# A two-layer hybrid decoder trunk on one core: the last weight sum of the seven-product jobs is made on VectorE instead of by accumulating transfers

## The chip, the cores and the metric

The kernel runs on one core of one Trainium2 chip. The metric is the device time of one execution in microseconds; lower is better. Three runs of the kernel before took 1253.19, 1253.20 and 1253.69 us, the median is 1253.2 us. A separate execution was taken with the hardware profiler.

## The reference

Two layers over a sequence of 256 tokens of width 1024, all in 32-bit floats. A layer normalizes h, makes one wide projection, runs retention (four heads) and a state-space scan (four groups) on its parts, projects both back, merges them by sigmoid gates, projects again and adds to h; a SwiGLU feed-forward of width 2816 follows. Cut to the products that matter here:

```python
u = h @ w_in                          # q, k, v, g_ret, z, xbc, dt, gate_ret, gate_ssd
yr = silu(g_ret) * norm(retention(rotary(q), rotary(k), v));  o_ret = yr @ ret_out
ys = norm((ssd_scan(...) + d_skip * xs) * silu(z)) * ssd_norm_w;  o_ssd = ys @ ssd_out
h = h + (sigmoid(gate_ret) * o_ret + sigmoid(gate_ssd) * o_ssd) @ w_o
gate, up = split(rmsnorm(h) @ w_gate_up)
h = h + (silu(gate) * up) @ w_down
```

## The kernel before, in words

**Weights in two parts.** Every large product is made in a 32-bit format of reduced precision, so each operand is split into a high part and a remainder, and three matmuls stand for one (`mm3`, lines 543 to 545). A weight piece is 128 rows by 1024 columns of numbers (512 KB). It is brought by a transfer from SyncE's queue (line 488) into one of four `raw` buffers, ScalarE copies it to `wh` (line 506), VectorE makes `wl = raw - wh` (line 527), and TensorE uses both. Seven pairs of `wh` and `wl` exist, so the splits run at most seven pieces ahead of TensorE. A piece of a plain job feeds 12 matmuls, a piece of a seven-product job 6.

**Seven products.** Some jobs compute a product of two matrices, cut into 2 x 2 blocks, by seven block products in place of eight. Besides the blocks 11, 22 and 21 of the weights they need four sums: t1 and t2 (made one after the other in the buffer of block 11), t3 (in the buffer of block 12) and t4, which adds block 21 to what t2 left. Each block is two pieces, so each sum is made twice in a job. The order of the products is 11, t1, t2, 22, t3, 21, t4, with the pieces of the job's other products (`"*"`) between them. Which sums are made by an accumulating transfer is said by `added`: for a name in it, `plus` calls `add` (line 416), in which GpSimd issues a transfer that reads block 21 again from memory and adds it to the buffer; for a name not in it VectorE adds the piece that is already on the chip (`tt`, line 230), and the piece's own buffer is freed only after that sum.

**The jobs.** Each layer has six such jobs: one for the state-space gate (`gs`, t3 added by transfer), the retention's out projection (`ret`, buffers called `dec`), the state space's (`ssd`), two gate-and-up jobs of the feed-forward and the down projection (buffers called `raws`, blocks 12 in `cc`). Around them stand plain jobs (`z`: 512 columns of the gate of the state space) and jobs in which the weight is the stationary operand (`fm`, lines 988 to 991).

**What sets the order.** The kernel plans itself while it is built: `Flow` runs all streams through a timetable with a cost for each operation, and the instructions are written to each engine in the order that this gives. A line that changes a stream can therefore move instructions of every engine. On the chip each engine works through its own list, and semaphores hold it until operands are there.

Of the kernel before, what the change touches and what calls it, by code (L numbers as in the profile page):

```python
# [192 lines left out]
def trunk_kernel(  # L193
# [58 lines left out]
    def pooled(pool_, shape, dt, tag, bufs):  # L252
        sem = Sem(bufs)
        return sem, lambda name=tag: pool_.tile(list(shape), dt, tag=tag, name=name, bufs=bufs)
# [5 lines left out]
    ccS, new_cc = pooled(tp, (P, D), F32, "cc", 2)  # L260
# [33 lines left out]
    AMID = ("*", "*", "*", "*", "11", "*", "t1", "*", "t2", "22", "*", "t3", "*", "21", "*", "t4")  # L294
# [4 lines left out]
    RMID = ('*', '*', '*', '*', '*', '*', '11', '*', 't1', 't2', '22', 't3', '21', 't4')  # L299
    RET_FIRST, RET_APART, RET_PR = (decS, new_dec), (), 0.0  # L300
# [5 lines left out]
    def group(*adds):  # L306

        of = len(jobs)
        got_turns, got_specs, stars = [], [], []
        for add in adds:  # L310
            t, f, at = add(of)
            if stars:

                t, f = ([(stars[i] if i < len(stars) else 1.0 + i, v) for i, (_, v) in enumerate(e)] for e in (t, f))
            stars = stars or at
            got_turns += t
            got_specs += f
        for into, got in ((turns, got_turns), (specs, got_specs)):
            for _, v in sorted(got, key=lambda e: e[0]):
                if into is turns and turns:  # L320
                    v.before = turns[-1]
                into.append(v)

    def plain(*runs):

        def add(of):
            got_turns, got_specs, n = [], [], sum(len(srcs) for srcs, _ in runs)
            for srcs, apart in runs:
                evs = []
                for i, (src, k, m) in enumerate(srcs):  # L330
                    ev, turn, at = Event(), Turn(), (len(got_turns) + 0.5) / n
                    evs.append(ev)
                    got_turns.append((at, turn))
                    slot = (bigS["D"], new_raw_big) if of == 0 and i < 4 else (rawS, new_raw)
                    got_specs.append((at, (src, k, m, of, slot,
                                           splitter(turn, k, m, ev, of, src if i in apart else None, slot[0]))))
                jobs.append(evs)
            return got_turns, got_specs, []
        return add
# [19 lines left out]
    def sevens(w1, w2, added=("t3",), order=ALONE, slots=None, first=None):  # L359

        def add(of):
            evs = {q: [Event(), Event()] for q in order if q != "*"}
            turn = {(q, i): Turn() for q in evs for i in range(2)}
            at = {(q, i): (2 * order.index(q) + i + 0.5) / (2 * len(order)) for q, i in turn}
            held = {(q, i): Event() for q in ("11", "12", "22", "21") for i in range(2)}
            part = {q: [w[k + i] for i in range(2)]
                    for q, k, w in (("11", 0, w1), ("12", 0, w2), ("22", 2, w2), ("21", 2, w1))}  # L370
            zS, new_z = slots or (rawS, new_raw)
            got_specs = []
            for q, need, sl in (("11", ("11",), first or (segS, new_raw_seg)), ("12", ("t1", "t3"), (zS, new_z)),
                                ("22", ("t2", "22"), (rawS, new_raw)), ("21", ("21",), (rawS, new_raw))):
                need = [c for c in need if c not in added or c not in ("t1", "t2")]
                for i in range(2):
                    land = holder(held[q, i])
                    if (q, i) == ("11", 1):
                        land = then(land, [wino_sums(i, of, evs, turn, held, part, added, zS, (first or (segS,))[0]) for i in range(2)])
                    got_specs.append((min(at[c, i] for c in need) - (0.01 if q == "12" else 0),  # L380
                                      (part[q][i], 2, 512, of, sl, land)))
            jobs.append(evs)
            return ([(at[c], turn[c]) for c in turn], got_specs,
                    [(i + 0.5) / len(order) for i, q in enumerate(order) if q == "*"])
        return add
# [7 lines left out]
    def holder(ev):  # L393
        def land(raw, landed):
            yield landed
            fl.set(ev, raw)
        return land

    def then(land, gens):
        def run(raw, landed):  # L400
            for g in gens:
                fl.spawn(g)
            yield from land(raw, landed)
        return run
# [56 lines left out]
    def tm_srcs(w, kper=2):  # L461

        n = w.shape[2] // 2
        return [(w[k // 2][:, (k % 2) * n : (k % 2 + kper) * n], kper, n) for k in range(0, 8, kper)]

    def fm_srcs(w):
        return [(w[i], 4, 256) for i in range(2)]

    def gate_up_srcs(l, c):
        return [tm_srcs(w_gate_up[l, b, c]) for b in range(2)]  # L470

    def gf_srcs(l, c):
        return [fm_srcs(w_gf[l, n + b]) for n in gf_at(c) for b in range(2)]

    def out_srcs(w):
        return [(w[k0 : k0 + P, :], 1, D) for k0 in range(0, w.shape[0], P)]
# [580 lines left out]
    def out_wino(op, nk, at, tag, order, post, add, ops):  # L1057
# [74 lines left out]
        for t in range(NT):  # L1132
# [8 lines left out]

    FFN = [[("plain", 0)],
           [("fm", 1)],
           [("seven", (2,), ("t3", "t4"))],
           [("fm", 3)],
           [("seven", (4,), ("t3", "t4"))],
           [("fm", NPAIR)]]
    DIRECT = ()
    DOWN_APART = ()
# [15 lines left out]
    def add_layer_jobs(l):  # L1165
        def srcs_of(kind, *at):
            if kind == "gr":
                return tm_srcs(w_gr[l, at[0]])
            if kind in FM:
                return fm_srcs(w_fm[l, FM[kind] + at[0] + (at[0] + at[1] if len(at) > 1 else 0)])  # L1170
            if kind in ("ret", "ssd", "wo"):
                return out_srcs({"ret": ret_out, "ssd": ssd_out, "wo": w_o}[kind][l])
            return tm_srcs(w_tm[l, TM[kind] + at[0]], kper=1 if l == 0 and (kind, *at) == ("v", 0) else 2)

        def adds_of(kind, *at, order=MIXED):
            if kind == "seven":
                c = TM[at[0]] + at[1]
                return [sevens(w_tm[l, c], w_tm[l, c + 1], added=at[2], order=order, slots=None)]
            return [plain((srcs_of(kind, *at), APARTS.get((kind, *at), ())))]

        for m in MIXERS[l]:
            if m == ("ret",):
                group(sevens(w_rw[l, 0], w_rw[l, 1], added=("t3", "t4"), order=RMID, first=RET_FIRST),
                      plain((out_srcs(ret_out[l])[8:], RET_APART)))
            elif m == ("ssd",):
                group(sevens(w_sw[l, 0], w_sw[l, 1], added=("t3", "t4"), order=SMID, slots=(ccS, new_cc)),
                      plain((out_srcs(ssd_out[l])[8:], ())))
            elif isinstance(m, tuple):
                for add in adds_of(*m, order=ALONE):
                    group(add)  # L1190
            else:
                group(*(chain(*(a for j in stream for a in adds_of(*j))) for stream in m))
        for members in FFN:
            adds = []
            for kind, *at in members:
                if kind == "seven":
                    adds.append(chain(*(sevens(w_gate_up[l, 0, c], w_gate_up[l, 1, c], added=at[1], order=ALONE if len(members) == 1 else ASIDE,
                                               slots=(ccS, new_cc)) for c in at[0])))
                elif kind == "fm":
                    adds.append(plain(*((srcs, APART) for c in at for srcs in gf_srcs(l, c))))  # L1200
                else:
                    adds.append(plain(*((srcs, APART) for c in at for srcs in gate_up_srcs(l, c))))
            group(*adds)
        lone = [s for k, s in enumerate(out_srcs(w_down[l])) if k // 4 not in (DW, DW + 1)]
        group(sevens(w_dw[l, 0], w_dw[l, 1], added=("t3", "t4"), order=AMID, slots=(ccS, new_cc)),
              plain((lone, DOWN_APART)))

    def params(l, done):
# [852 lines left out]
    for l in range(DEPTH):  # L2061
        add_layer_jobs(l)
# [158 lines left out]
```

## Time and profile before

| | |
|---|---|
| median of the runs | 1253.2 us |
| the profiled execution | 1253.21 us |
| its span, first to last instruction | 1251.4 us |
| TensorE busy (matmuls) | 1241.9 us, 99% |
| VectorE busy | 1108.2 us, 89% |
| ScalarE busy | 882.7 us, 71% |
| GpSimd busy | 71.1 us, 6% |
| transfers | 266.27 MB, mean 213 GB/s |
| software queue (GpSimd's transfers) | 27.38 MB, 11.8% of the 16 engines' time |
| granted TensorE clock | 0.999 of 2.4 GHz |

Busy time is the time in which an engine had an instruction in work. TensorE's matmuls are pipelined and their ends are modelled, so its 99% says that it was hardly ever without work, not that each matmul was as short as can be. The chain of waits goes back from the last instruction to whatever released each step. In a timeline row the first number is the start, the second the time until the end of the last of the xN instructions.

### The profile page before, as it was taken

How to read it: one execution, taken by the hardware profiler on the slowest of the kernel's cores; microseconds unless marked ns; L12 is line 12 of the kernel's file. 1: busy time of each engine (PE TensorE's matmuls, PEld its weight loads, DVE VectorE, ACT ScalarE, POOL GpSimd, SP SyncE). 2: the span in 40 equal slices, each digit the busy share in tenths (PEclk: the TensorE clock that was granted, in tenths of full speed). 3: DMA queues.
4: the chain of work that ended last, by engine and by line, in shares of the span. 5: the costliest groups of instructions: out<-in, count | busy, mean ns of one | idle time of the engine just before them, and what ended most of it. 6: DMA issues, size and time to landing. Idle time of an engine off the chain costs nothing.

```text
span 1251.4 us, 17609 instructions
## 1 busy us (share of the span) xinstructions
PE 1241.9 (99%) x6286; PEld 1052.4 (84%) x6286; DVE 1108.2 (89%) x1516; ACT 882.7 (71%) x1305; POOL 71.1 (6%) x92
## 2 busy tenths in 40 slices
PE   9999999999999999999999999999999999999997
PEld 8889888888888888888888898888888888888886
DVE  6998989789999979999788888888899998899995
ACT  6866876977776666776586676878877674776753
POOL 0000000001012001001000000000010110010000
PEclk9999999999999999999999999999999999999999
DMA  8758555456768658877776475555577786688872
GB/s 293 248 146 284 184 180 174 153 194 192 253 238 226 229 178 231 297 212 219 249 257 227 124 256 167 188 172 163 208 186 234 243 234 213 225 209 249 289 204 86
DMA packets 76343, 266.27 MB, mean 213 GB/s; under 512 B 8768, under 2 KB 9024, under 8 KB 76256
## 3 DMA queue, kind: packets, MB, share of 16 engines
q1 hardware_dynamic: 68416, 237.25, 55.7%
q0 software_dynamic: 7552, 27.38, 11.8%
q8 instruction: 49, 0.80, 0.2%
q10 hardware_dynamic: 288, 0.52, 0.1%
q14 instruction: 38, 0.31, 0.1%
HBM read 262.96 MB, written 2.16 MB: 212 GB/s over the span
## 4 chain that ended last, share of the span: by engine, by line
PE 92%; ACT 3%; issue 2%; DMA 1%; DVE 0%; POOL 0%; SPq 0%; POOLq 0%; ACTq 0%
PE acc L543 19%; PE acc L544 19%; PE acc L545 19%; PE acc L988 15%; PE acc L989 9%; PE tr L640 2%; PE yps L1700 2%; PE acc L991 2%; ACT wh L506 1%; ACT seg L1668 1%; PE acc L1422 1%; PE tr L1593 1%; PE ips L1687 1%; DMA raw<-in_w_tm_dram 1%; DMA raw<-in_w_gr_dram 0%
## 5 line engine op out<-in xcount | busy, mean ns | idle before, releaser
L506 ACT ACTIVATE wh<-raw 128x1024 fp32r<-128x1024 f32 (+2 forms) x388 | 397.0, 1035 | 150.6 <-PE acc L545 36.3
L527 DVE TENSOR_TENSOR wl<-raw,wh 128x1024 fp32r<-128x1024 f32 (+2 forms) x388 | 458.9, 1196 | 48.5 <-ACT wh L506 46.6
L988 PE MATMUL acc<-xT,wh 128*128 128x512 f32 x840 | 304.2, 400 | 0.0
L989 PE MATMUL acc<-xT,wl 128*128 128x256 f32 x960 | 251.6, 281 | 0.0
L543 PE MATMUL acc<-wh,xT 128*128 128x512 f32 (+1 forms) x568 | 220.6, 388 | 0.0
L545 PE MATMUL acc<-wh,xT 128*128 128x512 f32 (+1 forms) x568 | 216.1, 380 | 0.0
L544 PE MATMUL acc<-wl,xT 128*128 128x512 f32 (+1 forms) x568 | 216.1, 380 | 0.0
L989 PEld LDWEIGHTS acc<-xT,wl 128*128 128x128 f32 x960 | 181.2, 189 | 10.1
L988 PEld LDWEIGHTS acc<-xT,wh 128*128 128x128 f32 x840 | 158.0, 188 | 32.2
L544 PEld LDWEIGHTS acc<-wl,xT 128*128 128x128 f32 x568 | 106.7, 188 | 20.4 <-issue 1.2
L543 PEld LDWEIGHTS acc<-wh,xT 128*128 128x128 f32 x568 | 106.7, 188 | 19.8 <-issue 1.6
L545 PEld LDWEIGHTS acc<-wh,xT 128*128 128x128 f32 x568 | 106.6, 188 | 19.5
L506 ACT ACTIVATE wh<-raws 128x1024 fp32r<-128x1024 f32 x80 | 83.5, 1056 | 31.7 <-DVE raws L230 12.5
L527 DVE TENSOR_TENSOR wl<-raws,wh 128x1024 fp32r<-128x1024 f32 x80 | 96.4, 1222 | 8.9 <-ACT wh L506 8.7
L543 PE MATMUL acc<-wh,A 128*128 128x512 f32 x224 | 89.8, 401 | 0.2
L545 PE MATMUL acc<-wh,A 128*128 128x512 f32 x224 | 87.4, 390 | 0.0
L544 PE MATMUL acc<-wl,A 128*128 128x512 f32 x224 | 87.3, 390 | 0.0
L233 DVE SCALAR_TENSOR_TENSOR cc<-cc,cv 128x255 f32<-128x255 f32 (+1 forms) x144 | 67.3, 479 | 3.0 <-ACT cc L223 2.1
L543 PE MATMUL acc<-wh,C 128*128 128x512 f32 (+1 forms) x152 | 59.2, 389 | 0.0
L544 PE MATMUL acc<-wl,C 128*128 128x512 f32 (+1 forms) x152 | 58.3, 384 | 0.2 <-DVE wl L527 0.2
L545 PE MATMUL acc<-wh,C 128*128 128x512 f32 (+1 forms) x152 | 58.2, 383 | 0.0
L223 ACT ACT_TABLE_LOAD x41 | 52.6, 1283 | 6.1 <-DVE cc L233 5.4
(197 smaller groups left out, 2006.8 us busy)
## 6 DMA issues: line engine op xcount, KB each, us to landing
raw<-in_w_tm_dram SPq DMA_DIRECT2D x104, 512.0 KB, 4.2
raw<-in_w_fm_dram SPq DMA_DIRECT2D x80, 512.0 KB, 4.3
raw<-in_w_gf_dram SPq DMA_DIRECT2D x40, 512.0 KB, 4.5
raw<-in_w_gate_up_dram SPq DMA_DIRECT2D x32, 512.0 KB, 5.8
raw<-in_w_down_dram SPq DMA_DIRECT2D x28, 512.0 KB, 4.5
raw<-in_w_gr_dram SPq DMA_DIRECT2D x24, 352.0 KB, 3.7
seg<-acs SPq DMA_DIRECT2D x16, 512.0 KB, 4.9
raw<-in_ret_out_dram SPq DMA_DIRECT2D x16, 512.0 KB, 4.3
```

The lines of the kernel that those rows point to most:

```text
L223: return Op("act", cost, lambda: nc.scalar.activation(out=out, in_=in_, func=func, **kw), pr, TABLES.get(func))
L233: return Op("dve", 1.04 * n + 130, lambda: nc.vector.scalar_tensor_tensor(out=out, in0=in0, scalar=scalar, in1=in1, op0=op0, op1=op1), pr)
L506: nc.scalar.activation(out=wh[:, :m], in_=raw[:, :m], func=AF.Copy)
L527: nc.vector.tensor_tensor(out=wl[:, :m], in0=raw[:, :m], in1=wh[:, :m].bitcast(F32), op=ALU.subtract)
L543: nc.tensor.matmul(ps, lhsT=lh, rhs=rh, start=first, stop=False, **kw)
L544: nc.tensor.matmul(ps, lhsT=lh, rhs=rl, start=False, stop=False, **kw)
L545: nc.tensor.matmul(ps, lhsT=ll, rhs=rh, start=False, stop=last, **kw)
L640: nc.tensor.transpose(out=ps[:, j * P : (j + 1) * P], in_=src[:, j * P : (j + 1) * P], identity=ident)
L988: nc.tensor.matmul(a, lhsT=wh[:, k % 4, fsl], rhs=x[:, k % 4, :, :], start=k == 0, stop=False)
L989: nc.tensor.matmul(a[:, :SEQ], lhsT=wl[:, k % 4, fsl], rhs=xh[:, k % 4, :], start=False, stop=False)
L991: nc.tensor.matmul(a, lhsT=wh[:, k % 4, fsl], rhs=x[:, k % 4, :, :], start=False, stop=True)
L1700: nc.tensor.matmul(ps[:, i * HD : (i + 1) * HD], lhsT=sg[:, i, :], rhs=xdt[:, i * HD : (i + 1) * HD], start=True, stop=True)
```

## The change

In four of the six seven-product jobs of a layer t4 leaves the tuple `added`: the two gate-and-up jobs, the retention's out projection and the down projection. The state space's out projection keeps both, and the gate job of the state space had t3 alone already.

```diff
     FFN = [[("plain", 0)],
            [("fm", 1)],
-           [("seven", (2,), ("t3", "t4"))],
+           [("seven", (2,), ("t3",))],
            [("fm", 3)],
-           [("seven", (4,), ("t3", "t4"))],
+           [("seven", (4,), ("t3",))],
            [("fm", NPAIR)]]
...
             if m == ("ret",):
-                group(sevens(w_rw[l, 0], w_rw[l, 1], added=("t3", "t4"), order=RMID, first=RET_FIRST),
+                group(sevens(w_rw[l, 0], w_rw[l, 1], added=("t3",), order=RMID, first=RET_FIRST),
                       plain((out_srcs(ret_out[l])[8:], RET_APART)))
...
-        group(sevens(w_dw[l, 0], w_dw[l, 1], added=("t3", "t4"), order=AMID, slots=(ccS, new_cc)),
+        group(sevens(w_dw[l, 0], w_dw[l, 1], added=("t3",), order=AMID, slots=(ccS, new_cc)),
               plain((lone, DOWN_APART)))
```

The 16 transfers of t4 go from GpSimd's list, and VectorE's has 16 sums more. The planner moves other instructions too; TensorE's work is the same, some of it in another order.

VectorE in the first layer's retention out projection, before (-) and after (+): `dec` are the buffers of blocks 11, `raw` of the others, `seg`, `tail`, `xdt`, `yps` belong to the state-space scan that runs beside it, `O` and `sx` take the results.

```order
 L527 TENSOR_TENSOR wl<-raw,wh 128x1024
+L230 TENSOR_TENSOR dec<-dec,raw 128x1024
 L230 TENSOR_TENSOR tail<-tail,xdt 128x512
 L230 TENSOR_TENSOR O<-sx,D 128x512
...
+L230 TENSOR_TENSOR dec<-dec,raw 128x1024
+L527 TENSOR_TENSOR wl<-raw,wh 128x1024 x2
+L527 TENSOR_TENSOR wl<-dec,wh 128x1024 x2
 L230 TENSOR_TENSOR sx<-acc,sx 128x512
...
-L230 TENSOR_TENSOR seg<-seg,cbm 128x1024
```

The two sums come right after the last piece of t3, ahead of the splits of block 21 and of t4; the seg product moves behind the first four splits of the next job.

TensorE at the transposes of the first z result (`tr`), a job later, before:

```order
1556 L543 MATMUL acc_3474<-wh_3442,xT_342 128x512
1557 L544 MATMUL acc_3474<-wl_3457,xT_342 128x512
1558 L545 MATMUL acc_3474<-wh_3442,xT_342 128x512
1559 L640 MATMUL tr_3540<-cst_78,sil_3450 128x128 x4
1560 L543 MATMUL acc_3482<-wh_3442,xT_342 128x512
```

and after:

```order
1557 L545 MATMUL acc_3457<-wh_3440,xT_342 128x512
1558 L1700 MATMUL yps_3522<-xdt_3438,seg_3147 128x64 x8
1559 L543 MATMUL acc_3462<-wh_3440,xT_342 128x512
1560 L544 MATMUL acc_3462<-wl_3454,xT_342 128x512
1561 L545 MATMUL acc_3462<-wh_3440,xT_342 128x512
1562 L640 MATMUL tr_3542<-cst_78,sil_3447 128x128 x4
```

The scan's products `yps` stood earlier and are now just ahead of the transposes, which come three matmuls later.

VectorE in the first layer's down projection, from the second t2 sum's neighbours on (`raws` of blocks 11, `cc` of blocks 12, `O` is h), before:

```order
727 L527 TENSOR_TENSOR wl_5771<-raw_5575,wh_5752 128x1024
728 L527 TENSOR_TENSOR wl_5782<-raws_5490,wh_5763 128x1024
729 L527 TENSOR_TENSOR wl_5794<-raw_5553,wh_5773 128x1024
730 L527 TENSOR_TENSOR wl_5802<-raw_5686,wh_5786 128x1024
731 L527 TENSOR_TENSOR wl_5816<-cc_5513,wh_5797 128x1024
732 L527 TENSOR_TENSOR wl_5827<-cc_5520,wh_5804 128x1024
```

and after:

```order
732 L527 TENSOR_TENSOR wl_5775<-raw_5581,wh_5765 128x1024
733 L230 TENSOR_TENSOR O_3857<-O_3857,sx_5770 128x512
734 L527 TENSOR_TENSOR wl_5790<-raws_5509,wh_5777 128x1024
735 L527 TENSOR_TENSOR wl_5800<-raw_5563,wh_5788 128x1024
736 L527 TENSOR_TENSOR wl_5810<-raw_5679,wh_5795 128x1024
737 L527 TENSOR_TENSOR wl_5821<-cc_5525,wh_5805 128x1024
738 L527 TENSOR_TENSOR wl_5833<-cc_5532,wh_5814 128x1024
739 L230 TENSOR_TENSOR raws_5501<-raws_5501,raw_5786 128x1024
740 L527 TENSOR_TENSOR wl_5847<-raw_5741,wh_5828 128x1024
741 L527 TENSOR_TENSOR wl_5857<-raw_5786,wh_5835 128x1024
```

The first t4 sum stands behind the splits of t2, 22 and t3; an update of h has moved ahead of the second t2 split.

## Rows read from the trace of the kernel before

**Rows 1.** The page: TensorE's busy time, and the chain that ended last.
```profile
PE 1241.9 (99%) x6286; PEld 1052.4 (84%) x6286; DVE 1108.2 (89%) x1516; ACT 882.7 (71%) x1305; POOL 71.1 (6%) x92
...
PE 92%; ACT 3%; issue 2%; DMA 1%; DVE 0%; POOL 0%; SPq 0%; POOLq 0%; ACTq 0%
```

**Rows 2.** The waits of TensorE: us in total, times, longest us.
```profile
PE idle L2094 <- DVE mhalf L2071: 1.3, 1, 1.3
PE tr L640 <- DVE sil L233: 0.6, 2, 0.3
PE acc L544 <- DVE wl L527: 0.2, 1, 0.2
```

**Rows 3.** Groups by line and shape: busy us, mean ns, idle before.
```profile
L230 DVE TENSOR_TENSOR raws<-raws,raw 128x1024 f32<-128x1024 f32 x28 | 34.2, 1222 | 0.4 <-DMA raw<-in_w_tm_dram 0.4
...
L416 POOL DMA_DIRECT2D raws<-in_w_gate_up_dram x8 | 6.9, 863 | 32.1 <-DVE wl L527 21.3 <-DVE sx L230 10.8
```

**Rows 4.** Issues of transfers: KB each, median us from issue to landing.
```profile
raws<-in_w_gate_up_dram POOLq DMA_DIRECT2D x8, 512.0 KB, 5.5
...
raws<-in_w_dw_dram POOLq DMA_DIRECT2D x4, 512.0 KB, 6.7
```

**Rows 5.** Busy us in stretches: PE, PEld, DVE, ACT, POOL; clock, DMA share, GB/s.
```profile
290.00:366.00 76.00, 76.00 (x371) 63.15 (x370) 74.51 (x93) 55.07 (x79) 6.80 (x10) 1.00 0.72 221
496.00:518.00 22.00, 22.00 (x104) 18.45 (x103) 22.00 (x24) 17.96 (x22) 0.88 (x1) 1.00 0.83 244
...
600.00:620.00 20.00, 20.00 (x90) 16.57 (x89) 15.34 (x15) 12.05 (x13) 0.00 (x0) 1.00 0.78 259
```

**Rows 6.** Timeline of VectorE, retention's out projection and z: start us, us, [idle before].
```profile
315.34 0.69 DVE L230 TENSOR_TENSOR tail<-tail,xdt 128x512 f32<-128x512 f32 x1
316.55 0.69 DVE L230 TENSOR_TENSOR O<-sx,D 128x512 f32<-128x512 f32 x1 [0.52 <-PE acc L544]
...
329.49 0.69 DVE L230 TENSOR_TENSOR O<-acc,D 128x512 f32<-128x512 f32 x1 [0.17 <-PE acc L545]
...
335.05 4.63 DVE L527 TENSOR_TENSOR wl<-raw,wh 128x1024 fp32r<-128x1024 f32 x4
...
348.82 1.42 DVE L233 SCALAR_TENSOR_TENSOR sil<-sil,rz,wb 128x512 f32<-128x512 f32 x2
```

**Rows 7.** Timeline of TensorE where those results are used.
```profile
337.68 0.39 PE L544 MATMUL acc<-wl,xT 128*128 128x512 f32 x1
...
350.85 0.60 PE L640 MATMUL tr<-cst,sil 128*128 128x128 f32 x4
```

**Rows 8.** Block 21 in the retention's job, 309 to 313 us: its transfers.
```profile
L488 SPq DMA_DIRECT2D raw<-in_w_rw_dram x2: 327/328/328, 310.1 to 312.4; - x2
L416 POOL DMA_DIRECT2D dec<-in_w_rw_dram x1: 863/863/863, 311.5 to 311.5; - x1
...
DMA to landing us min/median/max: 4.4/6.8/7.0
```

**Rows 9.** Timeline of VectorE, a gate-and-up job and the down projection.
```profile
497.31 1.23 DVE L527 TENSOR_TENSOR wl<-raw,wh 128x1024 fp32r<-128x1024 f32 x1
...
568.45 1.23 DVE L230 TENSOR_TENSOR raws<-raws,cc 128x1024 f32<-128x1024 f32 x1 [1.93 <-DMA cc<-in_w_dw_dram]
...
590.03 1.23 DVE L527 TENSOR_TENSOR wl<-raws,wh 128x1024 fp32r<-128x1024 f32 x1
...
601.70 2.45 DVE L527 TENSOR_TENSOR wl<-raw,wh 128x1024 fp32r<-128x1024 f32 x2 [1.82 <-ACT wh L506]
```

**Rows 10.** Timeline of TensorE where these splits are used.
```profile
504.14 0.39 PE L544 MATMUL acc<-wl,D 128*128 128x512 f32 x1
...
592.49 0.39 PE L543 MATMUL acc<-wh,D 128*128 128x512 f32 x1
592.72 0.39 PE L544 MATMUL acc<-wl,D 128*128 128x512 f32 x1
```

## The prediction

> **What bounds the kernel now.** Read first the busy shares and the chain of waits on the page, then what TensorE waited for, then VectorE's groups, and last the timelines of the places where the change puts work. The profiled execution took 1253.21 us, its span is 1251.4, so 1.8 us lie around the span; the median of the runs is 1253.2, the same. TensorE is busy for 1241.9 us and the chain that ended last is 92% TensorE, 3% ScalarE and 0% VectorE [rows 1]. TensorE's named waits are three rows, 1.3 + 0.6 + 0.2 = 2.1 us, and the largest is the start [rows 2]. So the kernel is bound by TensorE's own work, which the change leaves alone. There is hardly a wait to win back. Time can be lost where VectorE, already full in stretches (74.51 of 76 us at the retention's out projection, 22.00 of 22 in a gate-and-up job) [rows 5], delivers a split weight later than TensorE asks for it. The question is therefore one of margins: how long before its first use each split weight is ready.
>
> **The change part by part.** Four jobs of each layer are touched: the retention's out projection, the two gate-and-up jobs and the down projection. Each has two t4 sums, so 2 x 4 x 2 = 16.
>
> Removed: 16 accumulating transfers of 512 KB, each issued by GpSimd in 0.86 us [rows 3] and landing 5.5 to 6.7 us after the issue (medians) [rows 4]. That is 8.4 MB of queue traffic and 13.8 us of GpSimd. Neither engine nor queue stands in TensorE's waits [rows 2], so I cost the removal at nothing; at most it can return part of those 2.1 us.
>
> Added: 16 VectorE sums of 1.22 us (the same instruction stands there for t2, `raws<-raws,raw`, mean 1222 ns) [rows 3], 16 x 1.222 = 19.6 us by duration. Back to back one occupies the engine for less: four splits of 1.23 take 4.63 us [rows 6], a pitch of (4.63 - 1.23) / 3 = 1.13. So a job gets 2.27 us of VectorE, all jobs 18.2 us. Its cost on the path is between 0 (all inside the margins) and 18.2 us (none); I take the margins of each place.
>
> Retention's out projection. The thinnest margin is the first weight of the next job: its split is the first of the four that start at 335.05, ready at 336.28, and TensorE takes it at 337.68 [rows 6, 7], a margin of 1.40. In the new order two sums come in ahead of it and one seg product, also of 1024 elements, goes behind it, net one pitch, 1.13 us. Two idle pieces of VectorE in that stretch end on TensorE's results, not on VectorE's own lateness: 0.52 before 316.55 and 0.17 before 329.49 [rows 6]. TensorE's schedule doesn't move, so the sums fill them. Net lateness 1.13 - 0.52 - 0.17 = 0.44, margin left 0.96, cost 0. If nothing filled them the lateness is 1.13, still inside 1.40; if the seg product had stayed in front as well, it is 2.27, and the stall is 0.87.
>
> Then the z jobs. The transposes of the first z result stand on TensorE at 350.85, and the two multiplications that feed them run from 348.82 to 350.24, the first done about 349.5 [rows 6, 7], a margin of about 1.3. Behind the four splits the seg product has been made up for, so VectorE is late by up to 2.27 - 0.69 = 1.58; the new TensorE order puts three more products ahead of these transposes, at 0.23 each (592.49 to 592.72) [rows 10] 0.69 us. Margin left 1.3 + 0.69 - 1.58 = 0.4, cost 0; with all 2.27 late, 0.3 of a stall.
>
> The gate-and-up jobs. After t2's splits the weight of product 22 is ready at 497.31 + 1.23 = 498.54 and used at 504.14 [rows 9, 10]: margin 5.6, and 2.27 goes into it. The t4 piece itself gains, since its sum no longer waits 5.5 us for a landing. Cost 0; the fm job behind it has only two weights to split and lets VectorE catch up.
>
> The down projection. The second t2 split starts at 590.03, is ready at 591.26 and used at 592.72 [rows 9, 10]: margin 1.46, the second thinnest place. The new t4 sums stand behind all t2, 22 and t3 splits, so they don't touch it; only one 512-wide update of h (0.69, as such updates take in the retention's stretch) [rows 6] comes ahead of it, margin left 0.77. Behind it VectorE now idles for 1.82 before 601.70 [rows 9] and for 4.66 of the 20 us from 600 to 620 (15.34 busy) [rows 5], which takes the 2.27. Cost 0.
>
> The sum is 1253.2 + 0 for eight jobs. Two places in each layer are left with under a microsecond by estimates that are good to about as much; I add 0.1 us for each of these four, 0.4 in all: **1253.6 us**.
>
> **One place where a rule is weighed.** The two pieces of w21 in the retention's job were issued at 310.1 and 312.4, with an accumulate between them; one of these three transfers took 4.4 us to land, the others 6.8 and 7.0 [rows 8]. The Trainium skill (DMA: Bandwidth & Descriptors, section SWDGE vs HWDGE vs iDMA) says that software-generated and hardware-generated transfers feed different queues of each DMA engine, which serves them in turn. By that rule the second plain transfer becomes faster without the accumulate beside it, near 4.4 us, and the sum stays as it is; by the row as it stands rival A gains. In numbers from rows: with 4.4 us the second piece is there at 316.8, with 6.8 at 319.2. The first new sum takes the place at 315.34, two updates of 512 follow (0.69 each) [rows 6], and the second sum is reached at 315.34 + 1.13 + 0.69 + 0.69 = 317.85, after the one landing and 1.35 us before the other. I take 4.4, as the accumulate is the only transfer that goes.
>
> **The rivals.**
>
> A, slower: the sum waits at the head of VectorE's queue. VectorE runs its queue in order, and a sum whose second operand has not landed holds every split behind it: the first t1 sum of the down projection had it idle for 1.93 us until a landing [rows 9]. The Trainium skill (TensorE: Matmul & The Clock Gate, section Architectural detail: the array is 16x 32x32) calls VectorE's queue a strict first-in, first-out; that row agrees. Place: the second t4 sum in the retention's job, and VectorE's lateness out of the second gate-and-up job running into the down projection. Price: in the retention 1.13 + 1.35 = 2.48 late (the idle pieces then move along) against 1.40, a stall of 1.08 a layer; in the down projection 2.27 brought along against 0.77, 1.50 a layer. Retention alone: 1253.2 + 2.2 = 1255.4; down projection alone: 1253.2 + 3.0 = 1256.2; both: 1258.4. It decides from a lateness of 1.40 and 0.77 us. For it: the full VectorE and the 6.8 us landing. Against it: the accumulate that shared the queue is gone, and the 1.93 idle ahead of the down projection swallows most of a lateness of 2.27.
>
> B, slightly slower: the splits hold, but VectorE's other results come late through the z jobs (the 0.4 us margin above, and the state-space results whose TensorE work moves by up to 6 us in the new order). Price: 0.3 to 1.2 us a layer, 1253.8 to 1255.6. For it: TensorE's row for tr already waits on VectorE's sil (0.6 us) [rows 2]. Against: that row is two waits of 0.3 at most, and no row tells of yps.
>
> C, faster: the freed queue brings later weights sooner, the t4 pieces are ready earlier, and part of TensorE's stalls goes. Price: at best the 0.6 + 0.2 us that aren't the start's, and about as much again in gaps too short to be named, 1252.0. Against it: no TensorE wait ends on a transfer [rows 2].
>
> **How the numbers follow.** The forecast (1252.8 to 1254.3) gets 0.64, A 0.18, B 0.13, C 0.05. The range 1252.6 to 1256.2 holds the forecast, B and the two lesser cases of A; above it stay A in both places (up to 0.08) and the sums hidden nowhere, below it C. No change means within 0.2%, 2.5 us, about what a measurement of this kernel can tell: the forecast, A in the retention alone, nearly all of B, and C fall there. Slower by more: A but for the retention alone, and the far end of B, 0.16 in all. Faster by more needs a gain of 2.5 us where the named waits are 2.1, 0.02. Same 0.82.
>
> **What would show it.** Right: 16 more 1.22 us sums on VectorE (40 of `raws<-raws,raw` in place of 28, and four more with `dec`), its busy time up by some 18 us, the software queue's share down by a third, TensorE's waits still two or three rows of a few tenths. A: a row in which TensorE waits for wl near 325 to 338 or 590 to 596 and the same places in the second layer, and a VectorE sum that waits for a landing of in_w_rw. B: TensorE's tr or yps waiting for VectorE's sil, xdt or seg between 340 and 400. The prediction is wrong if TensorE's matmuls themselves change pace, or if a stall over 0.9 us stands in any touched job.

## The result, and the profile after

The changed kernel takes 1257.0 us (median of nine executions, 1255.32 to 1258.43), the kernel before 1253.2 us beside it (nine, 1253.05 to 1254.39). The ratio is 1.0024, 95% interval 1.0015 to 1.0033: slower by 1.9 to 4.1 us. The forecast was 1253.6, and the range ended at 1256.2.

The profiled execution took 1255.32 us, the lowest of the nine; its span is 1253.6, 2.2 longer than before's. First the page: busy time and the chain that ended last, which answer to [rows 1].

```profile
PE 1243.3 (99%) x6286; PEld 1052.2 (84%) x6286; DVE 1122.0 (90%) x1532; ACT 880.7 (70%) x1305; POOL 66.6 (5%) x76
...
PE 83%; DVE 5%; ACT 4%; issue 4%; DMA 3%; POOL 0%; SPq 0%; POOLq 0%; DVEq 0%; ACTq 0%
```

The 16 sums are there (1516 VectorE instructions became 1532) and the 16 transfers are gone (92 on GpSimd became 76). VectorE's busy time is up by 13.8 us, where the prediction named some 18 as a sign of being right; GpSimd's is down by only 4.5, although 16 issues of 0.86 us are gone: other work on it takes longer (its powers, below). VectorE, absent from the chain before, now holds 5% of it. The waits of TensorE, which answer to [rows 2] (us in total, times, longest):

```profile
PE idle L2094 <- DVE mhalf L2071: 1.3, 1, 1.3
PE tr L640 <- DVE D L230: 1.1, 2, 0.6
PE tr L640 <- DVE sil L233: 0.5, 2, 0.3
```

New is the second row: transposes of `D`, the sums that VectorE makes behind the state space's out projection, one in each layer. To see where time goes, I set each matmul of both traces at its median spacing in the trace before and read how late TensorE is when it has done the same work ("at equal work" below means that this lateness is taken off). Between 300 and 440 us, from the retention's out projection to the end of the state space's, it becomes 1.35 us later; in the second layer, 954 to 1056, 1.00; at the down projection's first products (592, 1210) 0.1 and 0.0; elsewhere nothing. Two more profiles of the same kernel, 1257.18 and 1256.46 us, give 1.20 + 1.07 and 1.03 + 1.15 at the first place, and 0.03 + 1.89 and 1.38 + 0.52 at the second. So there are two losses: one of 2.2 to 2.4 us in every profile, and one of 0.1 to 1.9 that changes from execution to execution.

The first loss, as VectorE's timeline shows it in a z job (start, time to the end, [idle before]):

```profile
359.16 1.22 DVE L527 TENSOR_TENSOR wl<-raw,wh 128x1024 fp32r<-128x1024 f32 x1
359.33 1.46 POOL L243 TENSOR_TENSOR rz<-ms,mhalf 128x1 f32<-128x1 f32 x1 [9.20 <-DVE ms L238]
360.82 0.75 DVE L233 SCALAR_TENSOR_TENSOR sil<-sil,rz,wb 128x512 f32<-128x512 f32 x1 [0.44 <-POOL rz L243]
...
361.72 1.46 POOL L243 TENSOR_TENSOR rz<-ms,mhalf 128x1 f32<-128x1 f32 x1 [0.93 <-DVE ms L238]
363.21 0.75 DVE L233 SCALAR_TENSOR_TENSOR sil<-sil,rz,wb 128x512 f32<-128x512 f32 x1 [0.44 <-POOL rz L243]
```

The same job before, where two moments went together, an update with `ips` from the accumulators stood behind them, and the two scalings came without a wait:

```profile
360.09 0.69 DVE L230 TENSOR_TENSOR xdt<-ips,sr 128x512 f32<-128x512 f32 x1
360.19 1.06 POOL L243 TENSOR_TENSOR rz<-ms,mhalf 128x1 f32<-128x1 f32 x2 [10.87 <-DVE ms L238]
360.78 1.42 DVE L233 SCALAR_TENSOR_TENSOR sil<-sil,rz,wb 128x512 f32<-128x512 f32 x2
```

`rz` is a power of one number per row, made on GpSimd from the moment `ms`; VectorE scales z with it. In the new order the scaling stands one weight split behind its moment, and VectorE, first in line, waits for GpSimd. From 290 to 432 us VectorE's waits are, before and then after:

```profile
DVE wl L527 <- ACT wh L506: 0.7, 2, 0.5
DVE O L230 <- PE acc L544: 0.5, 1, 0.5
DVE sil L230 <- ACT sil L223: 0.3, 1, 0.3
DVE C L230 <- PE yps L1700: 0.2, 1, 0.2
DVE O L230 <- PE acc L545: 0.2, 1, 0.2
```

```profile
DVE sil L233 <- POOL rz L243: 2.1, 5, 0.5
DVE wl L527 <- ACT wh L506: 0.8, 1, 0.8
DVE C L230 <- PE yps L1700: 0.2, 1, 0.2
```

The two idle pieces that I meant the sums to fill (`O`, 0.5 and 0.2) [rows 6] are filled; five waits for GpSimd, 2.1 us, are new. What comes of them at the end of the state space's job, in the changed kernel:

```profile
401.60 0.86 POOL L416 DMA_DIRECT2D raws<-in_w_sw_dram  x1 [1.41 <-issue]
...
411.56 1.23 DVE L527 TENSOR_TENSOR wl<-raws,wh 128x1024 fp32r<-128x1024 f32 x1 [0.80 <-ACT wh L506]
...
422.05 0.69 DVE L230 TENSOR_TENSOR D<-D 128x512 f32<-128x512 f32 x1
...
422.89 0.63 PE L640 MATMUL tr<-cst,D 128*128 128x128 f32 x4 [0.57 <-DVE D L230]
```

VectorE's splits of t2 come late, so the state space's own accumulate goes out at 401.60, VectorE idles 0.80 for it (through ScalarE's copy of it), and the update that the transposes wait for starts at 422.05. Before, these two were

```profile
398.31 0.86 POOL L416 DMA_DIRECT2D raws<-in_w_sw_dram  x1 [0.17 <-issue]
...
419.84 0.69 DVE L230 TENSOR_TENSOR D<-D 128x512 f32<-128x512 f32 x1
```

The second loss is read from SyncE's queue and VectorE's splits. Before, then after (the third column of a row is the queue or the engine; a row's time runs over all its issues):

```profile
552.57 4.93 SPq L488 DMA_DIRECT2D raw<-in_w_down_dram  x4
...
555.92 1.22 DVE L527 TENSOR_TENSOR wl<-raw,wh 128x1024 fp32r<-128x1024 f32 x1
...
557.55 0.90 SPq L488 DMA_DIRECT2D raws<-in_w_dw_dram  x2
...
559.28 1.23 SPq L488 DMA_DIRECT2D cc<-in_w_dw_dram  x2
```

```profile
554.41 6.17 SPq L488 DMA_DIRECT2D raw<-in_w_down_dram  x4
...
558.95 1.23 DVE L527 TENSOR_TENSOR wl<-raw,wh 128x1024 fp32r<-128x1024 f32 x1
...
560.62 0.90 SPq L488 DMA_DIRECT2D raws<-in_w_dw_dram  x2
...
562.32 0.97 SPq L488 DMA_DIRECT2D cc<-in_w_dw_dram  x2
```

SyncE's list is the same there in both: four plain pieces stand ahead of the down projection's blocks. But each of these pieces goes out when a split of VectorE has freed a `raw` buffer (the last at 557.17 before, 0.03 us behind the split of 555.92; at 560.24 after, behind that of 558.95). The splits come late out of the second gate-and-up job, where the first split behind both new sums starts at

```profile
542.87 2.36 DVE L527 TENSOR_TENSOR wl<-raw,wh 128x1024 fp32r<-128x1024 f32 x2
```

and its counterpart before at 539.76, 3.1 us earlier, 1.8 at equal work. VectorE doesn't make this up, and the blocks go out 3.1 us later, 1.8 at equal work. The first t1 sum, which waited for its block until 568.45 before, and the second t2 split, which started at 590.03 [rows 9], are now

```profile
570.89 1.23 DVE L230 TENSOR_TENSOR raws<-raws,cc 128x1024 f32<-128x1024 f32 x1 [1.19 <-DMA cc<-in_w_dw_dram]
...
592.75 1.22 DVE L527 TENSOR_TENSOR wl<-raws,wh 128x1024 fp32r<-128x1024 f32 x1
```

2.4 and 2.7 us later, at equal work 1.1 and 1.4: nearly the whole margin of 1.46 that stood there is used, and this execution got through with 0.1 lost. The third profile (1256.46 us), with its blocks 2.8 us later at equal work, did not:

```profile
591.97 0.50 PE L543 MATMUL acc<-wh,D 128*128 128x512 f32 x1 [0.16 <-ACT sx L223]
...
594.49 0.50 PE L544 MATMUL acc<-wl,D 128*128 128x512 f32 x1 [0.61 <-DVE wl L527]
```

Over the two layers of the three profiles, blocks that go out 1.8 to 2.0 us later at equal work go with a loss of 0.0 to 0.5 there, and 2.8 and 3.2 us with 1.4 and 1.9. This chain is read from traces; no run here changes one of its links alone, and why the lateness differs between executions stays open.

Behind the down job, where VectorE had 4.66 us to spare [rows 5], the sums took 4.08 of it (15.34 to 19.42 busy), at no cost:

```profile
600.00:620.00 20.00, 20.00 (x90) 16.53 (x90) 19.42 (x20) 11.24 (x13) 0.00 (x0) 1.00 0.72 238
```

### The profile page after: what moved, and what is told of

Read it like the earlier page. It is cut to its first block, busy times and chain, and to the rows that moved or that the text cites. A ratio compares the mean times of both kernels' runs of the same rounds, so it can differ in the third digit from the quotient of the medians.

```text
span 1253.6 us, 17555 instructions
## 1 busy us (share of the span) xinstructions
PE 1243.3 (99%) x6286; PEld 1052.2 (84%) x6286; DVE 1122.0 (90%) x1532; ACT 880.7 (70%) x1305; POOL 66.6 (5%) x76
## 4 chain that ended last, share of the span: by engine, by line
PE 83%; DVE 5%; ACT 4%; issue 4%; DMA 3%; POOL 0%; SPq 0%; POOLq 0%; DVEq 0%; ACTq 0%
PE acc L543 17%; PE acc L544 17%; PE acc L545 17%; PE acc L988 14%; PE acc L989 8%; DVE wl L527 3%; PE yps L1700 2%; PE tr L640 2%; PE acc L991 2%; ACT wh L506 2%; DMA raws<-in_w_sw_dram 1%; DMA raw<-in_w_tm_dram 1%; ACT seg L1668 1%; PE ips L1687 1%; PE tr L1593 1%
```

## The experiments

Each was timed beside the kernel before; a ratio has its 95% interval, and "lost" is TensorE's lateness in the run's profile, first + second layer, at the retention-to-state-space place (R) and at the down projection (D).

**Which job costs: e1, e2, e13, e12.** The retention's sums alone, both feed-forward products', the gate-and-up's, the down projection's. Each is the kernel before with a part of the change, here e1's:

```diff
-                group(sevens(w_rw[l, 0], w_rw[l, 1], added=("t3", "t4"), order=RMID, first=RET_FIRST),
+                group(sevens(w_rw[l, 0], w_rw[l, 1], added=("t3",), order=RMID, first=RET_FIRST),
```

> The kernel before with the fourth sums of the retention's product alone made on VectorE (four of 1.13 us, two in each layer); all other products keep their adding transfers. Load theory (VectorE is full from 290 to 430 us, so what the retention adds there is carried through to the state space's transposes and ends there): the whole loss, 1255.5 to 1258 us, with TensorE late first at about 421 us in layer 0 and 1040 us in layer 1. Rival, the feed-forward's products carry the loss or a half of it: 1253.2 to 1254.5 us.

> The kernel before with the fourth sums of the gate-and-up and down products on VectorE, and the retention's by adding transfers as before. Load theory: no loss, 1252.8 to 1253.7 us, since VectorE has idle time in these stages. Rival, the feed-forward's products carry a part of the loss: 1254.5 to 1256 us, with a wait of TensorE on VectorE's splits or of VectorE on ScalarE's casts there that before does not have.

> The kernel before with the fourth sums of the gate-and-up jobs alone on VectorE. Open is the 0.4 to 1.0 us that TensorE loses at 592 or 1210 us, in the first products of the down projection, in the profiles of the versions with the feed-forward's sums. If VectorE is late out of the gate-and-up jobs, or the down projection's weights are issued later behind them, it stands here too: 1253.8 to 1255 us, with a wait of TensorE on a split at 592 or 1210 us. If it is the down projection's own new order: 1253.0 to 1253.6 us and no such wait.

> The kernel before with the fourth sums of the down projection alone on VectorE. The other side of the same question: its own new order at 592 and 1210 us gives 1253.8 to 1255 us and a wait of TensorE on a split there; lateness brought along from the gate-and-up jobs gives 1253.0 to 1253.6 us and no such wait.

| run | median us | ratio | lost at R | lost at D |
|---|---|---|---|---|
| e1, retention alone | 1256.06 | 1.0021 [1.0012, 1.0030] | 0.73 + 1.21 | 0.33 + 0.00 |
| e2, feed-forward alone | 1254.69 | 1.0007 [0.9998, 1.0016] | 0 + 0 | 0.75 + 0.00 |
| e13, gate-and-up alone | 1254.83 | 1.0009 [1.0001, 1.0018] | 0 + 0 | 1.06 + 0.35 |
| e12, down alone | 1253.36 | 0.9996 [0.9987, 1.0005] | 0 + 0 | 0 + 0 |

The retention has most of the loss, 2.6 us by its ratio. e2's median lies in the rival's band, not in that of "no loss"; its interval holds both (the kernel before took 1253.78 beside it), and its profile has a stall of 0.75. e13 and e12 place that: it belongs to the gate-and-up jobs' sums, though it is paid in the job behind; the down projection's own sums are free. A profile can lose 0.33 at D without any of this (e1 here, e5 below), so a single profile's loss there is good to no better. 0.0021 + 0.0009 - 0.0004 = 0.0026, and the whole change has 0.0024.

**The sums' time or the order: e6.** The theory I came with was that VectorE is full and the retention's sums are too much for it. e6 is e1 with each of the four sums cut to two columns; the order stays the same, instruction for instruction.

```diff
-                yield tt(D, pr, x, x, w, ALU.add)
+                yield tt(D, pr, *((a[:, :2] if q == "t4" and xS is not segS else a) for a in (x, x, w)), ALU.add)
```

> The version with the retention's fourth sums alone on VectorE, where each of these four sums covers two columns in place of 1024 and the rest of the sum is left out; the instructions, their order on every engine, their waits and the transfers are the same. Load theory (the 4 x 1.13 us on VectorE are the price): the loss of 2.3 us is gone, 1252.8 to 1254.2 us, no wait of TensorE at the state space's transposes near 421 us. Rival, the new order or the missing transfers: the loss stays, 1255.3 to 1256.5 us.

1256.12 us, 1.0018 [1.0009, 1.0026], lost at R 1.03 + 1.42: the loss stays without the sums' time. The load theory falls. VectorE's waits from 290 to 432 us:

```profile
DVE sil L233 <- POOL rz L243: 2.1, 5, 0.5
DVE wl L527 <- ACT wh L506: 1.1, 2, 0.6
DVE O L230 <- PE acc L544: 0.4, 1, 0.4
DVE O L230 <- PE acc L545: 0.4, 1, 0.4
```

Most of the freed time comes back as idle time ahead of the z jobs (the two `O` rows are waits for TensorE; VectorE is busy for 67.66 of the 70 us from 290 to 360, in e1 for 69.57), and the five waits for GpSimd behind it are 2.1 us as in the changed kernel (1.7 in e1).

**Those waits: e14, e9, e10.** The power is left out and `ms` handed on in its place, with its slot in the plan kept, so that the order is the same: e14 is e1 so treated, e9 the changed kernel, e10 the kernel before.

```diff
-                rz = yield from power(ms, 1, j, "rz", 6)
+                rz = yield Op("pool", 470, lambda: ms, j)
```

> The version with the retention's fourth sums alone on VectorE (loss 2.3 us), in the same order, with GpSimd's 16 powers of the z jobs left out of the computation. If the retention's loss is VectorE's waits for these powers, all of it goes: 1252.8 to 1254.0 us, and at equal work TensorE is no more than 0.2 us later than before between 360 and 430 us and between 980 and 1050 us. If a part of it is where the new order puts other work: 1254.3 to 1255.5 us.

> The changed kernel with the same order on every engine, but without GpSimd's 16 powers of the z jobs (rz from ms): VectorE scales with ms itself, so the power is left out of the computation. Wait theory (in the new order VectorE's scaling stands one place behind the moment and waits for GpSimd, 5 times and 2.1 us in each layer, and this is the loss): the waits are gone, 1252.8 to 1254.4 us, no wait of TensorE at the state space's transposes near 421 and 1040 us. Rival, the lateness comes from where the new order puts the splits and sums of the state space (its second sum 2.8 to 3.4 us later): the loss stays, 1255.5 to 1257.5 us.

> The kernel before with the same order, and the same 16 powers left out. Both theories: no change, 1252.8 to 1253.8 us, since before has no wait of VectorE on them from 290 to 430 us and TensorE does not wait there. If it gains more than 1 us, the powers cost in some way that the waits do not show, and what leaving them out gives the changed kernel has to be measured against this.

e14: 1253.84 us, 0.9998 [0.9989, 1.0007], lost at R 0.27 + 0.12. e9: 1254.48 us, 1.0007 [0.9998, 1.0015], lost at R 0.04 + 0.04 and at D 1.04 + 0.00. e10: 1253.07 us, 1.0000 [0.9992, 1.0009]. So the retention's loss is these waits: when they go it goes too, with the sums and the new order still there, and the kernel before gains nothing by the same. e14's ratio leaves nothing of it, its profile 0.39 us of e1's 1.94 (0.27 in one layer, where 0.2 was expected at most). These runs also take the powers out of the way of GpSimd's transfers; of VectorE's waits in the changed kernel from 290 to 432 us only the one of 0.80 ends on such a transfer, and e3 shows that it isn't the price. What e9 has left, 0.08 us above its band's end, is e2's.

**Another order for the scalings: e11.** The planner's cost of the power raised from 470 to 1000 and to 2000 ns, nothing left out.

```diff
-                rz = yield from power(ms, 1, j, "rz", 6)
+                rz = yield from power(ms, 1, j, "rz", 6, 1000)
```

> The changed kernel with the planner's cost of these powers raised from 470 to 1000 ns, so that it writes the order with more work between a moment and the scaling behind it. Wait theory: fewer waits of VectorE on GpSimd and a part of the loss back, 1253 to 1256 us. Rival (the new order's splits): 1255.5 to 1257.5 us.

> The same with 2000 ns, which the longest of these powers takes in the changed kernel's profile. Wait theory: no waits of VectorE on GpSimd, 1252.8 to 1254.5 us, unless the scaling itself then comes late for TensorE's z transposes, which would show as a wait of a transpose on the scaled tile near 350 to 395 us. Rival: 1255.5 to 1257.5 us.

1255.58 us, 1.0015 [1.0006, 1.0024], lost at R 0.49 + 0.56, at D 0.63 + 0.90; and 1254.78 us, 1.0011 [1.0002, 1.0020], lost at R 0.21 + 0.03, at D 0.35 + 1.09. Both have fewer waits than the changed kernel's 2.1 us (0.4 and 0.9 us of them from 290 to 432 us) and a smaller loss at R, but between the two the loss doesn't follow the waits, and the first lies in the bands of both theories. The powers are not shorter (medians 1398 and 1806 ns, 1428 in the changed kernel); more work stands between them and the scalings. The second was to have no such waits; it missed its band's end by 0.3, by the down projection's part.

**More sums and other sums: e3, e4.** The state space's fourth sums on VectorE too; and in the retention the second sum by transfer in the fourth's place.

```diff
-                group(sevens(w_sw[l, 0], w_sw[l, 1], added=("t3", "t4"), order=SMID, slots=(ccS, new_cc)),
+                group(sevens(w_sw[l, 0], w_sw[l, 1], added=("t3",), order=SMID, slots=(ccS, new_cc)),
```

```diff
-                group(sevens(w_rw[l, 0], w_rw[l, 1], added=("t3",), order=RMID, first=RET_FIRST),
+                group(sevens(w_rw[l, 0], w_rw[l, 1], added=("t2", "t3"), order=RMID, first=RET_FIRST),
```

> The changed kernel, and the state space's fourth sums made on VectorE too, so that no fourth sum goes by a transfer. Load theory with VectorE's own time alone as the price: two more sums of 1.13 us per layer in the stretch that is full, 1258 to 1261 us. Rival, what VectorE waits for at about 411 us (the state space's adding transfer, that lands late after the retention has delayed it: 8.8 us in the profile of the changed kernel) is the price: that wait is gone, 1253 to 1256 us, and the runs lie closer together than the changed kernel's 3.1 us.

> The changed kernel, but in the retention the second sum goes by an adding transfer in the fourth's place, so VectorE makes two sums in the retention as in the kernel before, with the order of the work planned anew. Load theory: 1252.8 to 1254 us, VectorE's idle time from 290 to 430 us back at about 2.6 us per layer or more. Rival, the loss is that of the fourth sum itself (its wait for the last transfer, or the order that follows from its being on VectorE): 1255 to 1257 us.

e3: 1258.64 us, 1.0044 [1.0031, 1.0056], lost at R 2.09 + 1.89. Without the state space's late accumulate the loss is not smaller but larger, so that transfer is a link of the chain in the changed kernel, not its price; the five waits of 2.1 us are here too. The time lies in the load theory's band (1258 to 1261), and TensorE now waits on splits (3.5 us, 6 times) and not on transposes of `D`; what the further loss comes from no run separates. e4: 1272.88 us, 1.0154 [1.0140, 1.0168], outside both expectations. Its chain of waits in the first layer (start, us) begins

```profile
300.57 9.92 DMA dec<-in_w_rw_dram
...
314.00 5.29 DMA raw<-in_w_rw_dram
```

and TensorE stands still for 3.4 us until 338.6. The second sum is needed early, and its transfer lands 9.92 us after it begins. e4 tells nothing of the theories, only what t2 by transfer costs here.

**VectorE's time by itself: e7, e5, e8.** The kernel before, order and transfers unchanged, with 8, 16 or 32 idle sums of two columns behind each second split of the retention.

```diff
+        spent = lambda: (yield Op("dve", 0.0, lambda: [nc.vector.tensor_tensor(out=junk, in0=mhalf, in1=mhalf, op=ALU.add) for _ in idle], pr))
-        yield from split(x, "t2")
+        yield from split(x, "t2"); yield from (spent() if idle else ())
```

> The same with 8 idle sums in place of 16, 1 to 2.5 us in each layer. Load theory with no slack at all in the full stretch: half the loss of 16. With a slack that takes about a microsecond first: less than half, 1253.2 to 1255 us. Order or transfers: no loss.

> The kernel before, every transfer and every order as they were, with 16 idle sums of two columns (about 0.07 to 0.15 us each) put on VectorE behind each of the retention's four second splits, so 2 to 5 us more VectorE time in each layer. Load theory: a loss as in the changed kernel or more, 1255 to 1260 us, taken at the state space's transposes (421 and 1040 us). Rival, order or transfers: no loss, 1253 to 1254 us.

> The same with 32 idle sums, 4 to 10 us in each layer. Load theory: beyond the slack each microsecond of VectorE costs TensorE a microsecond, so the step from 16 to 32 costs about the added VectorE time of both layers. If the lateness is partly made up in other ways: well under that. Order or transfers: no loss.

The group in e5 (count | busy us, mean ns):

```profile
L407 DVE TENSOR_TENSOR junk<-mhalf 128x2 f32<-128x2 f32 x64 | 10.3, 161 | 2.1
```

So 5.1, 10.3 and 20.6 us are added in all. They cost 1.0032 [1.0020, 1.0045], 1.0076 [1.0062, 1.0090] and 1.0164 [1.0150, 1.0178], that is 4.0, 9.5 and 20.6 us: nearly one for one, and for 8 and 16 more than was expected (1253.2 to 1255 and 1255 to 1260 us against 1258.11 and 1262.61). But the place isn't the expected one: most of it is lost ahead of the z jobs (e5: 3.8 us between 300 and 354, 3.6 between 760 and 954), and TensorE's scan products `ips` wait for ScalarE's `sx` (e5: 4.0 us, 2 times), not its transposes of `D`. A block of idle work put where the planner doesn't know of it costs nearly all of its time; the real sums, put in by the plan, cost nothing that e6 and e1 can tell apart (1.0018 and 1.0021, each good to 0.0009). The two kinds of load can't stand for each other, and these runs, which alone would have spoken for the load theory, don't explain the changed kernel.

**The changed kernel again.** Two more profiled executions, without an edit, for the question why the median lies 1.7 us over the first profile.

> The changed kernel once more, for a second profile. Its first profile (1255.32 us) is the lowest of nine executions with a median of 1257.0. If the remainder is the down projection's first products, an execution near the median shows the same 2.3 us at the state space's transposes and 0.5 to 1 us at 592 and at 1210 us, where the first profile shows 0.1 and 0.0. If it is the start (before 145 us), the difference stands there.

> The changed kernel, a third profile, with the same expectation: the part at the transposes is the same within 0.3 us, and what differs from the first profile stands at 592 and 1210 us or ahead of 145 us.

1257.18 and 1256.46 us: R is the same within 0.2 in each layer but for 0.32 once, and D differs, 0.1, 1.9 and 1.9 us in the three profiles (the start differs by 0.7 at most). So D is where the executions part.

## Why the prediction was wrong

- **The removal, at nothing:** right. No run without the transfers gains (e12: 0.9996), and the sums never waited for a landing in the retention: the group of 12 `dec<-dec,raw` has 0.0 us of idle time ahead of it.
- **The thin place of the retention, 0.96 left:** right. TensorE's lateness between 330 and 354 us moves by under 0.1.
- **The z jobs: "Behind the four splits the seg product has been made up for, so VectorE is late by up to 2.27 - 0.69 = 1.58 ... cost 0". This step failed.** Its margin held where I looked, the first transposes (`sil` is still 0.5 us in two waits, against 0.6) [rows 2]. But I moved VectorE only by the time of the sums and kept its waits as they were. The new order also parts the moments from each other and puts each scaling closer behind its own, so VectorE takes 2.1 us of new waits for GpSimd in a stretch where it is full (74.51 of 76 us) [rows 5], and doesn't make them up for the next 60 us. e6 and e14 show it from both sides. GpSimd was set aside as standing in no wait of TensorE's, and its powers don't occur in the sum.
- **The gate-and-up jobs, at nothing:** right for these jobs, wrong for what comes behind them. The 2.27 went into the margin of 5.6, but "lets VectorE catch up" failed: VectorE still frees its buffers 0.5 to 1.8 us late at equal work behind the second job, and SyncE's transfers of the down projection's blocks go out as late. Measured: 0.0009 of the time, 0.3 to 1.1 us in a layer (e13); e12, without these sums, issues the blocks on time and loses nothing.
- **The down projection, margin 0.77 left:** its own change costs nothing, as said (e12). The margin was spent by the late block, a transfer that I had counted as fixed; the idle 1.93 ahead of it [rows 9], which I held against rival A, was itself the wait for that landing and moved with it.
- **The rivals.** A has its second place (592, 1210), its cause there (VectorE's lateness out of the second gate-and-up job) and a price near that named (1.50 a layer; 0.0 to 1.9 measured), though the lateness comes by way of the transfers and not along VectorE's queue; it hasn't its first place. B has the kind of the larger loss, VectorE's other results coming late in the z jobs, with 0.3 to 1.2 us a layer against 1.0 to 1.35, but named the z transposes and `yps`, one job too early. B and A's down part together would have been 1253.2 + 2.4 + 3.0 at their ends; I gave B 0.13, and no chance to both at once. C's 1252.0 doesn't follow from its own terms, 0.8 and as much again (1251.6); nothing rests on it.
- **The one rule weighed** (the piece of block 21 landing sooner): by its sense the second sum finds its block there, and the trace agrees: the two pieces land in 4.2 us (median), and no `dec` sum waits. It decided nothing.

## What to carry to other kernels

When a plan is written anew, compare the order of every engine around each wait across engines, not only around the work that is added: a result made elsewhere that was covered by a piece of other work costs a full wait once that piece moves. Idle time of an engine that ends on a transfer is no reserve if the same change can move the transfer, and a queue whose list is unchanged still issues later when the buffers that it waits for come free later. And to tell an instruction's time from its place, keep the order and shrink the instruction; adding idle time answers another question.

## What the runs showed of the hardware

GpSimd's power of one column isn't always 0.55 us. All 16, minimum, median and maximum in ns, before and then after:

```profile
L243 POOL TENSOR_TENSOR rz<-ms,mhalf x16: 547/564/1203, 348.2 to 1005.9; 128x1 f32<-128x1 f32 x16
```

```profile
L243 POOL TENSOR_TENSOR rz<-ms,mhalf x16: 542/1428/2001, 348.0 to 1008.2; 128x1 f32<-128x1 f32 x16
```

The short ones (about 0.55) start beside a VectorE instruction that has an operand in the accumulators (`xdt<-ips` at 360.09: 1.06 for two), just ahead of another one, or while VectorE waits. Of the eleven of 1.39 us or more in the changed kernel nine start 0.1 to 0.25 us behind one that reads two tiles of SBUF, the cores' own memory for tiles (`wl<-raw,wh` at 359.16, pitch 1.13), the two of 1.73 us during a scaling with a split right behind it; all end about 0.5 us after that work, or after a second such instruction where one follows at once (360.79 against 360.29). So the same power, behind the wrong neighbour, holds VectorE for another 0.44 us when the scaling is next. The Trainium skill (SBUF — State Buffer, section Who interferes with whom) says that a VectorE instruction with two SBUF inputs contends with a GpSimd instruction that reads SBUF, over a shared read interface, and that issue order decides which one blocks. The nine long rows agree. That a power which came first holds up VectorE isn't seen: before, an update with two SBUF inputs (`A<-plain,A`, 374.56) began 0.11 us into a power and took its usual 0.69. No run was made for this alone.
